# A decoder block: one weight's low half ordered behind the first pair's row maxima and the forget sums' copy, and 11 of 16 residual transfers issued by GpSimd

## The chip, the cores and the metric

The kernel runs on one core of a Trainium2 chip. Its time is the device time of one execution, in microseconds (us). A profiled execution is traced as well; its span is the time from the first to the last traced instruction.

The core's engines are named as in the profile: PE (TensorE, matrix products; PEld is its loading of the stationary operand), DVE (VectorE), ACT (ScalarE), POOL (GpSimd) and SP (SyncE, which here only issues DMAs). Each engine works through its own queue in order and waits for others by semaphores.

## The reference

One layer of a hybrid decoder block, in fp32, for one sequence of 256 tokens with 1024 channels:

```python
h = rms_norm(x, attn_norm_g)
proj = h @ w_in        # q, k, v of two branches (8 heads of 64 each), forget logits, gate logits
qa, ka = partial_rope(rms_norm(heads(qa))), partial_rope(rms_norm(heads(ka)))
o_a = moba_attention(qa, ka, va)                 # blocks of 256 keys
log_f = log_sigmoid(f_logit + b_forget); c = cumsum(log_f)
o_b = softmax(rms_norm(qb) @ rms_norm(kb).T / 8 + c[t] - c[s], causal) @ vb
gates = sigmoid(g_logit + b_gate)                # two branches of 1024
merged = gates[0] * (o_a @ w_branch_moba) + gates[1] * (o_b @ w_branch_fox)
x = x + merged @ w_out
h2 = rms_norm(x, ffn_norm_g)
u, g = split(h2 @ w_ffn_up)                      # 2 x 2816
x = x + (silu(causal_depthwise_conv3(g) + b) * u) @ w_ffn_down
```

With 256 tokens there is a single block of keys, so the MoBA branch is plain causal attention.

## The kernel before

**Weights in two halves.** Every product with a weight is made of two fp32r numbers for each fp32 number: a high half and a low half. A weight chunk is 1 MB. SP loads it in one DMA into a raw buffer (`raw`, three of them, L131). Each half of the chunk (1024 of its 2048 columns) is then split: ACT copies it to `whi` (L134), and DVE subtracts that from the raw chunk and writes `wlo` (L135). Three products (high·high, high·low, low·high) are summed in PSUM. The halves `whi` and `wlo` rotate through six buffers each.

**What sets the order.** PE works in the order in which the program is written. The orders of DVE, ACT, SP and POOL are made by the scheduler of the framework from the program's order, its dependences and its own estimates. `load(upto)` (L116) walks through a fixed list of chunks (the projections, then gate weights wg 0 to 7, then the branch, output and feed-forward weights) and emits loads and splits up to half number `upto`. `use(c, h)` (L143) is called by each product group for its weight; unless `state["hold"]` is set, it first calls `load` five halves (AHEAD) beyond its own. `state["behind"]` may name two instructions behind which the next splits' high and low half are ordered (`after`, L89): this adds an order on the queue, but no data.

**The stage around the first edit.** `project(n, ..)` (products L247) makes the n-th projection; its last argument picks quarters of it. In the old program `project(4, pk, 1)` is the second half of the second key projection. Behind it come `forget_c` (L359 to L370: four products with a constant matrix sum the log forget gates, DVE copies them out of their PSUM bank, L366, adds a constant, L367, and ACT's queue sends them out and back in by two DMAs, L369 and L370), and `scores(0, pair)`, three of the four pairs of heads of the first branch. A pair's scores are `first_half` (products L400) and `second_half` (L407; L413 for the forgetting branch), then `softmax` (L420 to L437): DVE takes the row maxima (L428), ACT the exponentials (L431), DVE the reciprocal (L433) and the scaling (L436). PSUM has eight banks, so products wait for whoever reads a bank out.

Behind that, `finish_qk` normalises the second queries and keys (reduction L262, small operations L200 to L205, final product L269), and `start_turn` (L288 to L299) turns them: DVE transposes 32 by 32 blocks (L293), and 16 DMAs of 32 KB, issued by POOL and SP in turn, move the blocks (L298). Then come `project(5)` (the second values), `gate(0)` (products into two banks, evacuated by DVE at L490), the turn of the first pairs' probabilities (`turn`, products L450, evacuations L440 and L452), and so on through the gates and the four pairs of the forgetting branch.

**The stage around the second edit.** Late in the kernel, `spread_x` (L729 to L732), called behind feed-forward tile 17, issues 16 DMAs that spread the turned residual `turned_x` into `x1`, 32 partitions at a time. `down` (L776 to L820) adds `x1` to the output products (L799 and L809) and stores. Behind these 16 on SP stand the last two loads of the down weights (`wd`, L131).

Of the kernel before, what the change touches and what calls it, by code (L numbers as in the profile page):

```python
# [30 lines left out]
RB, HB, AHEAD = 3, 6, 5  # L31
# [11 lines left out]
def decoder_block(ctx, tc, a, out):  # L43
    nc = tc.nc
# [6 lines left out]
    def T(shape, tag, bufs=1, dt=F32):  # L51
        return sb.tile(shape, dt, tag=tag, bufs=bufs, name=tag)
# [32 lines left out]
    pos = {c: i for i, c in enumerate(chunks)}  # L85
    split = {}
    state = {"next": 0, "raw": None, "ahead": AHEAD, "hold": False, "behind": None}

    def after(i, j):  # L89
        tc.add_manual_dep(i.ins, j.ins.name, mybir.DependencyInfo(mybir.DependencyClass.NoSync, mybir.DependencyReason.DATA), reason="order")  # L90

    def lead(p):

        for k in (2 * p, 2 * p + 1):
            nc.sync.dma_start(lt[:, k], a["lead"][k])
        hi = T([P, 1024], "whi", HB, F32R)
        lo = T([P, 1024], "wlo", HB, F32R)
        for j in range(2):
            w = lt[:, 2 * p + j, S:]
            s = slice(j * W4, (j + 1) * W4)  # L100
            low = split_x(2 * p + j)
            whi = nc.scalar.activation(hi[:, s], w, AF.Copy)  # L102
            after(nc.vector.tensor_tensor(lo[:, s], w, hi[:, s].bitcast(F32), op=ALU.subtract), low)  # L103
        split[("qkv", 0, p // 2), p % 2] = (hi, lo, whi)

    def home(n):

        slot = (n - state["base"] - AHEAD - 1) % (HB + 3) if AHEAD < state["ahead"] else 3
        if slot > 2:
            return T([P, 1024], "whi", HB, F32R), T([P, 1024], "wlo", HB, F32R)  # L110
        if slot == 2:
            return [T([P, 1024], "qn", 3, F32R) for _ in range(2)]
        both = T([P, 2, 1024], ("V", "bias")[slot], 1, F32R)
        return both[:, 0], both[:, 1]

    def load(upto):  # L116
        while state["next"] <= min(upto, 2 * len(chunks) - 1):
            i, h = divmod(state["next"], 2)
            state["next"] += 1
            if i < 2:  # L120
                lead(2 * i + h)
                continue
            c = chunks[i]
            if h == 0:
                w = 1024 if i == 2 else 2048
                src = a[c[0]]
                for j in (c[1] - (c[0] == "qkv"), *c[2:]):
                    src = src[j]
                raw = state["raw"] = T([P, 2048], "raw", RB)
                for j in range(2048 // w):  # L130
                    nc.sync.dma_start(raw[:, j * w:(j + 1) * w], src[:, j * w:(j + 1) * w])  # L131
            raw = state["raw"][:, h * 1024:(h + 1) * 1024]
            hi, lo = home(2 * i + h)
            whi = nc.scalar.activation(hi, raw, AF.Copy)  # L134
            wlo = nc.vector.tensor_tensor(lo, raw, hi.bitcast(F32), op=ALU.subtract)  # L135
            if state["behind"]:
                for i, j in zip((whi, wlo), state["behind"]):
                    if j:
                        after(i, j)
            split[c, h] = (hi, lo, whi)  # L140
            state["whi"] = whi

    def use(c, h):  # L143
        if not state["hold"]:
            load(2 * pos[c] + h + state["ahead"])
        return split.pop((c, h))[:2]
# [60 lines left out]
    def pairs(ap):  # L207
        return ap.rearrange("p (a t) -> p t a", a=2)
# [29 lines left out]
    def project(m, pt, h, quarters=(0, 1)):  # L238
        for hh in quarters:
            wh, wl = use(("qkv", m, h) if isinstance(m, int) else m, hh)  # L240
            for k2 in range(2):
                k = 4 * h + 2 * hh + k2
                rh, rl = (pairs(w[:, k2 * 512:(k2 + 1) * 512]) for w in (wh, wl))
                parts = ((xh, rh), (xl, rh), (xh, rl)) if m == 0 else ((xh, rh), (xh, rl), (xl, rh))
                for i, (lhs, rhs) in enumerate(parts):
                    for t in range(NT):
                        nc.tensor.matmul(pt[t], lhs[:, k, t * P:(t + 1) * P], rhs, start=(k == 0 and i == 0), stop=(k == KT - 1 and i == 2))  # L247
# [53 lines left out]
    def end_turn(raw, br, isk, behind=None):  # L301
        dst = T([P, 4, S], f"{'qk'[isk]}T{br}")
        gain = col(C_QG + 2 * br + isk)
        i = nc.scalar.activation(dst.rearrange("p d (c i) -> p d c i", i=32), raw, AF.Copy, scale=gain)
        if behind:
            after(i, behind)
        turned[br, isk] = dst
# [51 lines left out]
    def forget_c():  # L359
        lf = fg["lf"]  # L360
        cp = bank()
        c0, c1 = (cp[:NH, t * P:(t + 1) * P] for t in range(NT))
        for t, c in enumerate((c0, c1)):
            nc.tensor.matmul(c, lf[:, t], tri, start=True, stop=True)
        cT = T([P, 2, 384], "pT", 4)[:NH, 0, 0:S]
        nc.vector.tensor_copy(cT, cp[:NH, 0:S])  # L366
        nc.vector.tensor_scalar_add(cT[:, P:S], cT[:, P:S], cT[:, P - 1:P])  # L367
        cd = dr.tile([NH, S], F32, name="cd")
        nc.scalar.dma_start(cd, cT)  # L369
        nc.scalar.dma_start(bias[:, :, P:P + S], bass.AP(tensor=cd.tensor, offset=cd.offset, ap=[[0, P], [S, NH], [1, S]]))  # L370
# [12 lines left out]
    last_max = []  # L383
# [12 lines left out]
    def first_half(br, pair, sps=None):  # L396
        sps = sps or banks()
        for j in range(2):
            rows = parts[j][0]
            nc.tensor.matmul(sps[j][:, 0:P], turned[br, 0][rows, pair, 0:P], turned[br, 1][rows, pair, 0:P], start=True, stop=True)  # L400
        return sps

    def second_half(br, pair, sps):
        if br not in halved:
            for j in range(2):
                rows = parts[j][0]
                nc.tensor.matmul(sps[j][:, P:3 * P], turned[br, 0][rows, pair, P:S], turned[br, 1][rows, pair], start=True, stop=True)  # L407
            return
        qs, ks = halved[br]
        for i, (q, k) in enumerate(((0, 0), (0, 1), (1, 0))):  # L410
            for j in range(2):
                rows = parts[j][0]
                nc.tensor.matmul(sps[j][:, P:3 * P], qs[q][rows, pair], ks[k][rows, pair], start=(i == 0), stop=(i == 2))  # L413

    def scores(br, pair):
        sps = first_half(br, pair)
        second_half(br, pair, sps)
        softmax(br, pair, sps)

    def softmax(br, pair, sps):  # L420
        s = T([P, 2, 384], "s", 4)
        nm = T([P, 2, 2], "nm", 4)
        l = T([P, 2, 2], "l", 4)
        for j in range(2):
            h = 2 * pair + j
            sp = sps[j]
            for i, c in enumerate((slice(0, 128), slice(128, 384))):
                last_max[:] = [nc.vector.tensor_tensor_reduce(s[:, j, c], sp[:, c], mask3[:, c] if br == 0 else bias[:, h, c],  # L428
                                               scale=1.0, scalar=3e38, op0=ALU.add, op1=ALU.min, accum_out=nm[:, j, i:i + 1])]
            for i, c in enumerate((slice(0, 128), slice(128, 384))):  # L430
                last_exp[:] = [nc.scalar.activation(s[:, j, c], s[:, j, c], AF.Exp, scale=-1.0, bias=nm[:, j, i:i + 1], accum_out=l[:, j, i:i + 1])]  # L431
        r = T([P, 2, 2], "r", 4)
        nc.vector.reciprocal(r, l)  # L433
        for j in range(2):
            for i, c in enumerate((slice(0, 128), slice(128, 384))):
                last_norm[:] = [nc.vector.tensor_scalar_mul(s[:, j, c], s[:, j, c], r[:, j, i:i + 1])]  # L436
        probs[br, pair] = s  # L437
# [60 lines left out]
    def banks():  # L498
        return [bank() for _ in range(NT)]

    forget_a()
    pq, pk, pv = banks(), banks(), banks()
# [17 lines left out]
    pk = banks()  # L520
# [1 line left out]
    gate_bias()  # L522
    end_turn(q0, 0, 0)
    end_turn(k0, 0, 1)
    project(4, pk, 1)
    forget_c()
    for pair in range(3):
        scores(0, pair)
    q1 = start_turn(q1, 0, last_norm[0])
    k1 = start_turn(finish_qk(pk, 1, 1, last_max[0]), 1)  # L530
# [192 lines left out]
    x1 = lt[:, :, S:2 * S]  # L723
    turned_x = lt[:, :, 2 * S:3 * S]
# [4 lines left out]
    def spread_x():  # L729
        for r in range(4):  # L730
            for b in range(4):
                nc.sync.dma_start(x1[32 * b:32 * (b + 1), r::4], turned_x[32 * r:32 * (r + 1), b::4])  # L732


    acts = {}
# [175 lines left out]
```

## Time and profile before

| | us |
|---|---|
| the three runs | 349.32, 349.60, 349.99 |
| their median | 349.60 |
| the profiled execution | 350.03 |
| its span | 348.3 |

The profiled execution's own time is 1.7 us more than its span. In the profile's rows a line stands for one group of instructions on one engine: its start in us from the span's start, its length, engine and line of the kernel, operation, what it writes and reads (with partitions x elements), and how many there were. A bracket at the end says how long the engine stood idle before the group, and what it waited for. In the chain of waits each row is a start, a length and what ran; the chain is followed back from the last instruction to whatever released it. In the windows each engine has its busy time in a stretch and in brackets its number of instructions; PEclk is the clock that PE was granted, as a share of full speed. A DMA issue's row is the time that the issuing engine's queue spends on it, and the rows of DMA issues give the median from issue to landing.

The engines' shares, the stretch around the edit and the end of the kernel are shown in the prediction, where they are used.

### The profile page before, as it was taken

How to read it: one execution, taken by the hardware profiler on the slowest of the kernel's cores; microseconds unless marked ns; L12 is line 12 of the kernel's file. 1: busy time of each engine (PE TensorE's matmuls, PEld its weight loads, DVE VectorE, ACT ScalarE, POOL GpSimd, SP SyncE). 2: the span in 40 equal slices, each digit the busy share in tenths (PEclk: the TensorE clock that was granted, in tenths of full speed). 3: DMA queues.
4: the chain of work that ended last, by engine and by line, in shares of the span. 5: the costliest groups of instructions: out<-in, count | busy, mean ns of one | idle time of the engine just before them, and what ended most of it. 6: DMA issues, size and time to landing. Idle time of an engine off the chain costs nothing.

```text
span 348.3 us, 5440 instructions
## 1 busy us (share of the span) xinstructions
PE 342.0 (98%) x1983; PEld 299.8 (86%) x1983; DVE 297.1 (85%) x562; ACT 222.3 (64%) x384; POOL 18.3 (5%) x40
## 2 busy tenths in 40 slices
PE   8999999899999999999999999999999999999995
PEld 4878888788888888889999999989898999989884
DVE  4899998999979678998999999897978988797833
ACT  4967656877589575746767877574765674566320
POOL 0000161044000000000000000000000000000000
PEclk9999999999999999999999999999999999999999
DMA  7987859757940927575626656566465755545003
GB/s 263 413 344 255 296 157 312 280 157 210 350 170 6 340 60 250 194 275 207 243 74 289 208 170 243 226 243 218 147 239 166 241 199 196 191 102 237 2 0 121
DMA packets 17994, 72.19 MB, mean 207 GB/s; under 512 B 2856, under 2 KB 8112, under 8 KB 10544
## 3 DMA queue, kind: packets, MB, share of 16 engines
q1 hardware_dynamic: 15744, 69.74, 56.5%
q0 software_dynamic: 1024, 1.05, 1.3%
q10 hardware_dynamic: 1200, 1.06, 0.9%
q8 instruction: 15, 0.25, 0.3%
q14 instruction: 11, 0.09, 0.1%
HBM read 67.64 MB, written 1.06 MB: 197 GB/s over the span
## 4 chain that ended last, share of the span: by engine, by line
PE 81%; DMA 9%; DVE 4%; ACT 2%; SPq 2%; issue 1%; ACTq 0%
PE bank L647 26%; PE bank L786 16%; PE bank L247 15%; PE bank L648 13%; PE bank L598 6%; DMA raw<-in_qkv 6%; DVE wlo L135 2%; SPq L298 2%; PE bank L464 2%; DMA lead<-in_lead 1%; DMA raw<-in_wg 1%; ACT whi L134 1%; PE bank L450 1%; ACT qn L180 1%; PE bank L413 0%
## 5 line engine op out<-in xcount | busy, mean ns | idle before, releaser
L135 DVE TENSOR_TENSOR wlo<-raw,whi 128x1024 fp32r<-128x1024 f32 x94 | 113.9, 1220 | 9.6 <-ACT whi L134 9.1
L134 ACT ACTIVATE whi<-raw 128x1024 fp32r<-128x1024 f32 x94 | 97.9, 1053 | 25.9 <-PE bank L647 6.8
L247 PE MATMUL bank<-whi,x 128*128 128x512 f32 x320 | 84.1, 382 | 0.6 <-ACT whi L102 0.5
L647 PE MATMUL bank<-pp,whi 128*128 128x512 f32 x232 | 76.6, 382 | 0.0
L247 PEld LDWEIGHTS bank<-whi,x 128*128 128x128 f32 x320 | 60.0, 189 | 11.1 <-ACT whi L102 1.2
L648 PE MATMUL bank<-pp,wlo 128*128 128x256 f32 x232 | 63.3, 273 | 0.0
L647 PEld LDWEIGHTS bank<-pp,whi 128*128 128x128 f32 x232 | 43.9, 189 | 6.1
L247 PE MATMUL bank<-wlo,x 128*128 128x512 f32 x160 | 47.9, 381 | 0.0
L648 PEld LDWEIGHTS bank<-pp,wlo 128*128 128x128 f32 x232 | 44.6, 192 | 0.2
L247 PEld LDWEIGHTS bank<-wlo,x 128*128 128x128 f32 x160 | 30.0, 189 | 4.8 <-DVE wlo L103 0.8
L786 PE MATMUL bank<-whi,qT 128*128 128x512 f32 (+1 forms) x92 | 27.8, 371 | 0.0
L755 DVE TENSOR_TENSOR sq<-bank,lows 128x256 f32<-128x256 f32 x44 | 18.1, 417 | 8.7 <-ACT lows L754 8.6
L760 ACT ACTIVATE s<-sq,sm 128x256 f32<-128x256 f32 x22 | 13.1, 597 | 12.1 <-DVE sq L756 11.9
L754 ACT ACTIVATE lows<-bank 128x256 f32<-128x256 f32 x44 | 16.0, 369 | 7.2 <-PE bank L648 7.2
L298 POOL DMA_DIRECT2D pp<-pp x32 | 17.0, 540 | 47.4 <-DVE qf L268 22.9
L786 PEld LDWEIGHTS bank<-whi,qT 128*128 128x128 f32 x92 | 17.3, 190 | 2.3
L763 ACT ACTIVATE s<-s 128x256 f32<-128x256 f32 x22 | 9.1, 413 | 15.6 <-DVE s L762 15.5
L647 PE MATMUL bank<-pp,bias 128*128 128x512 f32 x56 | 18.7, 382 | 0.0
L786 PE MATMUL bank<-wlo,qT 128*128 128x512 f32 (+1 forms) x46 | 17.0, 370 | 0.0
L598 PE MATMUL bank<-whi,pp 128*128 128x512 f32 x64 | 17.0, 383 | 0.0
L756 DVE TENSOR_TENSOR sq<-sq,rsB 128x512 f32<-128x512 f32 x22 | 15.2, 691 | 0.5
L431 ACT ACTIVATE s<-s,nm 128x128 f32<-128x128 f32 (+1 forms) x32 | 14.2, 451 | 1.8 <-DVE nm L428 1.8
(180 smaller groups left out, 578.3 us busy)
## 6 DMA issues: line engine op xcount, KB each, us to landing
raw<-in_wu SPq DMA_DIRECT2D x22, 1024.0 KB, 4.8
raw<-in_wd SPq DMA_DIRECT2D x11, 1024.0 KB, 4.7
raw<-in_qkv SPq DMA_DIRECT2D x9, 1024.0 KB, 6.3
raw<-in_wg SPq DMA_DIRECT2D x8, 1024.0 KB, 5.4
raw<-in_wb SPq DMA_DIRECT2D x4, 1024.0 KB, 5.3
raw<-in_wo SPq DMA_DIRECT2D x4, 1024.0 KB, 4.8
lead<-in_lead SPq DMA_DIRECT2D x8, 384.0 KB, 6.5
raw<-in_qkv SPq DMA_DIRECT2D x2, 512.0 KB, 8.2
```

What stands on the lines that cost most here:

```text
L134: whi = nc.scalar.activation(hi, raw, AF.Copy)
L135: wlo = nc.vector.tensor_tensor(lo, raw, hi.bitcast(F32), op=ALU.subtract)
L247: nc.tensor.matmul(pt[t], lhs[:, k, t * P:(t + 1) * P], rhs, start=(k == 0 and i == 0), stop=(k == KT - 1 and i == 2))
L298: queues[r % len(queues)].dma_start(raw[32 * r:32 * (r + 1), :, b], y[32 * b:32 * (b + 1), r])
L431: last_exp[:] = [nc.scalar.activation(s[:, j, c], s[:, j, c], AF.Exp, scale=-1.0, bias=nm[:, j, i:i + 1], accum_out=l[:, j, i:i + 1])]
L598: nc.tensor.matmul(ps_[t], lhs[:, t * P:(t + 1) * P], rhs, start=(k == 0 and i == 0), stop=(k == 3 and i == 2))
L647: nc.tensor.matmul(two[i], wh[:, c], both, start=(k == 0), stop=False)
L648: nc.tensor.matmul(two[i][:, 0:S], wl[:, c], high, start=False, stop=(k == KT - 1))
L754: nc.scalar.activation(lows[:, i:i + 1].rearrange("p b (a t) -> p b a t", a=2), apart(two[i][:, S:2 * S], 1), AF.Copy)
L755: nc.vector.tensor_tensor(halves(ev[:, i:i + 1]), apart(two[i][:, 0:S], 1), halves(lows[:, i:i + 1]), op=ALU.add)
L756: nc.vector.tensor_tensor(ev, ev, rs2[:, None, :].to_broadcast([P, 2, S]), op=ALU.mult)
L786: nc.tensor.matmul(o, lhs, rhs, start=(first and i == 0), stop=(end and i == 2))
```

## The change

Two places are edited. In the first, the second half of `project(4, pk, 1)` is written in two quarters, and before the second the loading ahead is held. So the split that `use` would have emitted there (the first half of gate weight 0) is not emitted until `forget_c` and the first pair's scores are written. Then it is emitted by hand, with its low half ordered behind `last_max[0]`, the last of the first pair's row maxima. Nothing is computed that was not before. In the second, of the 16 DMAs of `spread_x` five stay with SP and 11 are issued by GpSimd.

```diff
     end_turn(k0, 0, 1)
-    project(4, pk, 1)
+    project(4, pk, 1, (0,))
+    state["hold"] = True
+    project(4, pk, 1, (1,))
     forget_c()
-    for pair in range(3):
+    scores(0, 0)
+    state["hold"], state["behind"] = False, (None, last_max[0])
+    load(2 * pos["qkv", 4, 1] + 1 + AHEAD)
+    state["behind"] = None
+    for pair in range(1, 3):
         scores(0, pair)
...
         for r in range(4):
             for b in range(4):
-                nc.sync.dma_start(x1[32 * b:32 * (b + 1), r::4], turned_x[32 * r:32 * (r + 1), b::4])
+                (nc.sync if b == 3 or r == b == 0 else nc.gpsimd).dma_start(x1[32 * b:32 * (b + 1), r::4], turned_x[32 * r:32 * (r + 1), b::4])
```

The scheduler makes DVE's new order from that. The first piece is DVE's queue ahead of the copy of the forget sums (L366; `pT` is the buffer it goes to). A row is a line, an operation, what it writes and reads, its tile, and the semaphores for which it waits:

```order
 L269 TENSOR_TENSOR qn<-bank,qf 128x512 [waits DVE_49] x2
 L135 TENSOR_TENSOR wlo<-raw,whi 128x1024 [waits Activation_49]
-L135 TENSOR_TENSOR wlo<-raw,whi 128x1024 [waits DMAHW1_49,Activation_49]
 L366 COPY pT<-bank 8x256 [waits PE_49]
 L367 TENSOR_SCALAR pT<-pT 8x128 [waits DVE_49]
```

One low half has left its place in front of the copy. The one that stays is that of the last projection weight.

It comes back behind the first pair's maxima, where the low half of the same chunk's second half stood, and that one moves on behind the reduction (L262) of the second keys' normalisation. The next piece is DVE's queue there; `l` and `r` are the softmax's sums and reciprocals, `ss` and `qfv` the normalisation's small tiles:

```order
 L428 ISA nm 128x1
 L262 TENSOR_REDUCE ss<-sq 128x8 x2
+L135 TENSOR_TENSOR wlo<-raw,whi 128x1024
+L433 RECIPROCAL r<-l 128x4 [waits Activation_49]
 L200 TENSOR_SCALAR qfv<-ss 128x16 [waits DVE_49]
-L433 RECIPROCAL r<-l 128x4 [waits Activation_49]
 L436 TENSOR_SCALAR s<-s,r 128x128 [waits DVE_49]
```

The second half's low half now stands behind the two reductions, and one softmax's reciprocal and the first small operation of the normalisation have changed places.

PE's order is the same before and after. The last piece is PE's queue at the first two score products of the forgetting branch behind `gate(0)` to `gate(3)`, with the numbers of the buffers, since a bank's number tells who must have left it:

```order
L450 MATMUL bank_1125<-cst_172,s_974 128x64
L400 MATMUL bank_1140<-kT1_1067,qT1_997 128x128 [waits DVE_49,Activation_49]
L400 MATMUL bank_1141<-kT1_1067,qT1_997 128x128 [waits DVE_49]
L400 MATMUL bank_1144<-kT1_1067,qT1_997 128x128 [waits DVE_49]
L400 MATMUL bank_1145<-kT1_1067,qT1_997 128x128 [waits Activation_49]
L413 MATMUL bank_1140<-qn_1070,qn_1069 128x256
```

Four products start the first and second pair, each in a bank of its own, and each waits for the engine that read that bank out last.

On the two queues of the second edit, the 16 issues on SP become five ahead of the two `wd` loads, and POOL, which had nothing behind its 32 transfers of the turns (L298), gets eleven.

## The prediction

> **What bounds the kernel now.** I read the page's busy times first, then the windows, then the chain of waits in order of time around the edit, and then each engine's timeline there.
>
> ```profile
> PE 342.0 (98%) x1983; PEld 299.8 (86%) x1983; DVE 297.1 (85%) x562; ACT 222.3 (64%) x384; POOL 18.3 (5%) x40
> ...
> core 0: us, PE busy (x) PEld busy (x) DVE busy (x) ACT busy (x) POOL busy (x), PEclk, DMA share, GB/s
> 62.42:95.45 33.03, 32.96 (x178) 28.05 (x178) 32.89 (x86) 23.59 (x53) 8.43 (x16) 1.00 0.75 241
> 95.45:123.60 28.15, 28.15 (x198) 24.09 (x196) 20.90 (x67) 20.95 (x52) 0.00 (x0) 1.00 0.46 170
> ```
>
> TensorE (PE) is busy for 342.0 of the 348.3 us, at full clock, so a gain must come out of the 6.3 us in which it is not, or out of products that start late. From 62.42 to 95.45 us VectorE (DVE) is just as full, 32.89 of 33.03 us. There two engines bound the stage at once. After 95.45 only PE does. The chain shows how that stage is entered:
>
> ```profile
> 59.55 1.07 ACT whi L134
> 60.64 1.23 DVE wlo L135
> 61.86 0.33 DVE pT L366
> 62.22 0.28 DVE pT L367
> ...
> 63.65 15.59 PE bank L247 x71
> ```
>
> These are start, length and what ran. A weight's high half (ACT, L134) is waited for by its low half (DVE, L135), which stands in front of the copy of the forget sums (L366) on DVE, and PE's product stream resumes only at 63.65. The timelines of PE and DVE say why:
>
> ```profile
> 58.98 0.60 PE L364 MATMUL bank<-cst,lf 128*8 128x128 f32 x4
> 59.84 0.60 PE L407 MATMUL bank<-kT,qT 64*128 64x256 f32 x4
> 60.92 0.38 PE L400 MATMUL bank<-kT,qT 64*128 64x128 f32 x2
> 62.24 0.37 PE L400 MATMUL bank<-kT,qT 64*128 64x128 f32 x1 [0.93 <-DVE pT L366]
> 79.98 0.44 PE L400 MATMUL bank<-kT,qT 64*128 64x128 f32 x4
> 80.79 0.70 PE L247 MATMUL bank<-whi,x 128*128 128x512 f32 x2
> ```
> ```profile
> 57.96 1.22 DVE L135 TENSOR_TENSOR wlo<-raw,whi 128x1024 fp32r<-128x1024 f32 x1
> 60.64 1.23 DVE L135 TENSOR_TENSOR wlo<-raw,whi 128x1024 fp32r<-128x1024 f32 x1 [1.46 <-ACT whi L134]
> 62.42 0.27 DVE L428 CUSTOM_DVE_ANT_0 s<-bank,cst 128x128 f32<-128x128 f32 x1
> 63.53 1.21 DVE L135 TENSOR_TENSOR wlo<-raw,whi 128x1024 fp32r<-128x1024 f32 x1
> 65.22 0.16 DVE L433 RECIPROCAL r<-l 128x4 f32<-128x4 f32 x1
> 67.87 1.26 DVE L262 TENSOR_REDUCE ss<-sq 128x8 f32<-128x512 f32 x2
> 69.16 0.17 DVE L200 TENSOR_SCALAR qfv<-ss 128x16 f32<-128x16 f32 x1
> ```
>
> The forget products end at 59.58, but DVE idles 1.46 us for a high half and then works on the low half. The copy therefore comes more than 2 us late, the third pair's second score product waits 0.93 us for the bank that it frees, and project(5)'s first two products wait for the first pair's row maxima (62.42 to 63.60).
>
> **The change, part by part.**
>
> **1. The low half moves behind (gain at the door).** Without it DVE is free at 57.96 + 1.22 = 59.18. The copy starts when the forget products end, 59.6, takes 0.4, the scalar add 0.2: 60.25. The first pair's scores end at 59.84 + 0.60 = 60.44, and its four maxima take 63.53 - 62.42 = 1.1: DVE lets project(5)'s second product go at about 61.65. PE, no longer held at the third pair, needs what the same eight products need later without a wait, 80.79 - 79.98 = 0.81: 60.92 + 0.81 = 61.73, and one product (15.59 / 72 = 0.22) later 61.95. Before, that product stood at 63.65. So PE runs 1.7 us earlier from here by PE's own rows, 2.0 by DVE's. Nothing is removed: the low half still costs its 1.2 us on DVE, and DVE is full up to 95.45. So the question is what DVE owes at the end of its full stretch.
>
> **2. What DVE owes.** The moved half (first half of gate weight 0) takes the place that the next one (its second half) had at 63.53, and that second half goes behind L262. From there on DVE has done the same work as before at each row. Its clock there depends on the waits in between. DVE reaches the first reciprocal (L433) early and waits for ScalarE's exponentials:
>
> ```profile
> 61.65 1.05 ACT L134 ACTIVATE whi<-raw 128x1024 fp32r<-128x1024 f32 x1
> 62.52 0.53 ACTq L369 DMA_DIRECT2D cd<-pT  x1
> 63.10 0.40 ACT L431 ACTIVATE s<-s,nm 128x128 f32<-128x128 f32 x1 [0.40 <-DVE nm L428]
> 64.78 0.18 ACT L431 ACTIVATION_READ_ACCUMULATOR s<-s,nm 128x1 f32 x1
> ```
>
> ACT cannot start them before its high half of 61.65 ends, 62.65. In the old kernel they waited until 63.10, behind the DMA issue of 62.52 to 63.05, which itself waited for the forget copy. Now that issue goes out while the high half runs. The four exponentials take 63.10 to 64.96, 1.86, so they end at 64.5 and the reciprocal runs then instead of at 65.22: 0.7 earlier. From there to L262 nothing changes (2.65 us). Behind it stands the extra low half, 1.2 us, less some 0.2 to 0.3, since the small waits between the reduction, L200 and L436 are now filled by it. DVE is then late by 1.2 - 0.7 - 0.3 = 0.2 us, and stays so, being full. Bounds: 0.1 (exponentials at once) and 0.5 (nothing filled). If the exponentials started no earlier than before, it would be 1.0.
>
> **3. Where DVE and PE meet again.**
>
> ```profile
> 94.31 1.22 DVE L135 TENSOR_TENSOR wlo<-raw,whi 128x1024 fp32r<-128x1024 f32 x1
> 96.42 0.75 DVE L490 SCALAR_TENSOR_TENSOR lead<-bank,rs,lows 128x512 f32<-128x512 f32 x1 [0.89 <-PE bank L247]
> ...
> 97.39 0.30 PEld L400 LDWEIGHTS bank<-kT,qT 64*128 64x128 f32 x3
> ...
> 124.27 0.87 ACT L440 ACTIVATE pT<-bank 128x384 f32<-128x384 f32 x2 [5.64 <-PE bank L450]
> ...
> 123.54 0.75 DVE L490 SCALAR_TENSOR_TENSOR lead<-bank,rs,lows 128x512 f32<-128x512 f32 x1 [3.65 <-PE bank L247]
> ```
>
> Before, DVE had 0.89 us to spare at 96.42: the gate evacuation (L490) waited for PE. PE's first scores of the second forgetting pair, the middle one of the three rows from 97.39, at 97.5, reuse the bank that L490's first instruction frees. With PE 1.7 to 2.0 early, DVE arrives last: 95.5 + 0.2 = 95.7, plus 0.75 is 96.4. PE's product moves from 97.5 to 96.4. **1.1 us is left**, 0.8 with DVE 0.5 late. At 123.5 and 124.3 both other engines wait for PE by 3.65 and 5.64 us, so what PE has gained by then shifts everything behind it.
>
> **4. The next raw load.** The second half frees its raw buffer, so gate weight 3's load, issued at 64.76, moves behind L262, to about 69.5.
>
> ```profile
> 64.76 0.33 SPq L131 DMA_DIRECT2D raw<-in_wg  x1
> ...
> 76.69 1.06 ACT L134 ACTIVATE whi<-raw 128x1024 fp32r<-128x1024 f32 x1 [0.60 <-PE bank L247]
> ...
> raw<-in_wg SPq DMA_DIRECT2D x8, 1024.0 KB, 5.4
> ```
>
> It lands at about 75, and its conversion, at 76.69 before, waited for PE and not for data. Nothing is queued behind it on ACT that PE needs before the turn at about 77.5. I take 0.
>
> **5. The residual transfers.**
>
> ```profile
> 301.05 10.94 SPq L732 DMA_DIRECT2D lead<-lead  x16
> 312.08 1.01 SPq L131 DMA_DIRECT2D raw<-in_wd  x2
> ...
> 79.69 4.21 POOL L298 DMA_DIRECT2D pp<-pp  x8 [2.09 <-issue]
> ...
> pp<-pp POOLq DMA_DIRECT2D x32, 32.0 KB, 3.7
> ...
> 329.09 0.68 DVE L799 TENSOR_TENSOR s<-bank,lead 128x512 f32<-128x512 f32 x1
> ...
> 333.00 0.42 DVE L755 TENSOR_TENSOR sq<-bank,lows 128x256 f32<-128x256 f32 x1 [2.89 <-ACT lows L754]
> ```
>
> SP is free after 5 x 0.68 = 3.4 us instead of 10.94, so the last two weight loads go out some 5 to 8 us earlier. PE has no wait in that stretch, so this earns 0. GpSimd (POOL) issues 11; the trace has no such transfer from it. Bounds: 4.21 / 8 = 0.53 us each as for its own (5.8 us), or SP's 0.68 (7.5 us). I take 0.53. With 3.7 to land they are in by 311, and L799 reads them first at 329.09. The cover is 18 us; cost 0.
>
> That row also speaks to a rule. POOL's 0.53 us were taken at 79.69 to 83.9, beside a VectorE that was busy without a break. The Trainium skill (SBUF — State Buffer, "SBUF: two separate sides") says that descriptors of a GpSimd DMA cannot be written while VectorE holds the port pair that the two share. The same page, under "A bandwidth-pool intuition that's wrong (but worth ruling out)", gives about 620 ns alone and about 3100 ns beside such an operation. By that, as an estimate from this page, the eleven would take 34 us and come after L799. The trace speaks against it for this kernel's VectorE work.
>
> **Sum.** 1.1 + 0 + 0: span 348.3 to 347.2, this execution 350.03 to 348.9. It was 0.4 above the median of 349.6, to which I apply the same 1.1: 348.5 us.
>
> **Rivals.**
>
> *The whole gain stays:* the bank of L490 is not what PE waits for, and 1.7 to 2.0 us survive: 347.6 to 347.9. For: only one row in the stretch ties PE to DVE. Against: the order of the program has that wait. 0.10.
>
> *DVE gives it all back:* the exponentials start no earlier, DVE is 1.0 or more late, and 0 to 0.6 is left: 349.0 to 349.6. For: DVE is full for 33 us, and a queue that full forgives nothing. Against: the 0.40 idle before 63.10. 0.20.
>
> *The change does not act:* PE's bank and maxima are held by something else and 63.65 stays: 349.6. Against: the 0.93 names L366. 0.05.
>
> *Slower: GpSimd starved beside VectorE.* In 300 to 330 VectorE runs 1.2 us low halves. If each issue waited for two of them, 0.53 + 2 x 1.22 = 3.0, the eleven end at 333 and land at 336.5; L799 sits at the head of VectorE's queue until then, 7.4 late, and the last activations behind it have 2.9 of slack (333.00): 4.5 lost, less 1.1: 353. It decides from (329.1 - 301.1 - 3.7) / 11 = 2.2 us per issue. Against: 0.53 in both stretches seen. 0.08.
>
> **How the numbers follow.** Forecast 0.57 (348.3 to 348.8), rivals 0.10, 0.20, 0.05, 0.08. This kernel's measurement can tell about 0.2%, 0.7 us, from no change. Forecast and whole gain are faster, the next two within it, the last slower: 0.67, 0.25, 0.08. The range 347.6 to 349.7 takes in everything from the whole gain to none and leaves out the starved case and a little noise, about 1 in 10.
>
> **What would show it.** Step 1: project(5) resumes at 61.7 to 61.95, and the 0.93 before L400 is gone. Step 2: the reciprocal at 64.5 with DVE idle before it, L293 and the first row-turn transfers within 0.5 us of where they were. Step 3: L490 at 95.7 with no idle before it, and a wait of PE on it near 96.4; if that wait is absent, the first rival holds. Step 5: eleven POOL issues in about 6 us, L799 without a wait. I am wrong if project(5) resumes after 63, if DVE is more than 1 us late at L293, or if L799 waits.

## The result and the profile after

| | before | after |
|---|---|---|
| median, us (12 runs each, side by side) | 349.65 | 347.86 |
| lowest and highest | 348.85, 352.38 | 347.28, 348.96 |
| profiled execution | 350.03 | 347.68 |
| its span | 348.3 | 345.9 |

The ratio is 0.9946, with a 95% interval of 0.9927 to 0.9964: the kernel is 1.3 to 2.6 us faster. The forecast was 348.5, and the time lies within the range of 347.6 to 349.7. Two executions, of 398.64 us (the kernel before, beside the second four experiments) and of 926.5 us (the transfers alone), are left out of all ratios. The two profiled executions differ by 2.4 us of span, more than the medians (1.79). Most of what follows is about why.

The busy times of the changed kernel and its windows (columns as before), moved to where the same products now stand:

```profile
PE 341.7 (99%) x1983; PEld 299.9 (87%) x1983; DVE 296.4 (86%) x562; ACT 220.5 (64%) x384; POOL 24.2 (7%) x51
```
```profile
61.73:94.79 33.06, 33.06 (x178) 28.33 (x176) 32.78 (x78) 23.14 (x53) 8.44 (x16) 1.00 0.72 240
94.79:121.88 27.09, 27.09 (x193) 23.40 (x192) 20.81 (x67) 20.96 (x52) 0.00 (x0) 1.00 0.48 176
```

PE works as long as before, at the same full clock, in a shorter span; only waiting has gone. VectorE (DVE) is still full in the first window, 32.78 of 33.06 us. The timelines of PE at the two places of the prediction, the door of project(5) and the first scores behind `gate(0)` to `gate(3)`:

```profile
59.03 0.60 PE L364 MATMUL bank<-cst,lf 128*8 128x128 f32 x4
...
61.20 0.60 PE L407 MATMUL bank<-kT,qT 64*128 64x256 f32 x4
61.73 0.70 PE L247 MATMUL bank<-whi,x 128*128 128x512 f32 x2
...
77.47 0.96 PE L450 MATMUL bank<-cst,s 64*128 64x64 f32 x24
...
95.61 0.73 PE L400 MATMUL bank<-kT,qT 64*128 64x128 f32 x7
```

No row here carries a bracket: the 0.93 us before L400 has gone, and so has the wait that stood in front of project(5). At 95.61 PE does not wait either, though the prediction had it wait for L490 until 96.4. VectorE's timeline has the other side:

```profile
59.67 0.41 DVE L366 COPY pT<-bank 8x256 f32<-8x256 f32 x1 [1.45 <-PE bank L364]
...
61.64 1.22 DVE L135 TENSOR_TENSOR wlo<-raw,whi 128x1024 fp32r<-128x1024 f32 x1
...
63.62 0.18 DVE L433 RECIPROCAL r<-l 128x4 f32<-128x4 f32 x1 [0.21 <-ACT s L431]
...
67.47 1.21 DVE L135 TENSOR_TENSOR wlo<-raw,whi 128x1024 fp32r<-128x1024 f32 x1
...
70.85 1.30 DVE L293 STREAM_TRANSPOSE pp<-qn 128x512 f32<-128x512 f32 x2
...
94.79 1.41 DVE L490 SCALAR_TENSOR_TENSOR lead<-bank,rs,lows 128x512 f32<-128x512 f32 x2
```

The copy (L366) now waits for the forget products alone, the moved low half follows the maxima at 61.64, and the next one the reduction at 67.47. That is the order that the change asked for. But the reciprocal is at 63.62, where 64.5 was predicted, and L490 at 94.79, where 95.7 was predicted: VectorE is 0.9 us earlier than I had worked out, and the two L490 have ended just in time for PE. The second surprise is the end of the kernel. From the start of the last addition (L819 before, L825 after) to the end of the span it took 348.3 - 344.34 = 3.96 us before and takes 345.9 - 342.62 = 3.28 now:

```profile
344.34 0.42 DVE L819 TENSOR_TENSOR s<-bank,s 128x256 f32<-128x256 f32 x1 [0.92 <-PE bank L786]
```
```profile
342.62 0.42 DVE L825 TENSOR_TENSOR s<-bank,s 128x256 f32<-128x256 f32 x1 [0.92 <-PE bank L792]
```

So the 2.4 us between the two spans are 1.72 in which PE is earlier all the way to that addition, and 0.68 behind it. The prediction had 1.1 and 0.

### The profile page after: what moved, and what is told of

The parts are those of the page before. It is cut to its first block, busy times and chain, and to the rows that moved or that the text cites. A ratio compares the mean times of both kernels' runs of the same rounds, so it can differ in the third digit from the quotient of the medians.

```text
span 345.9 us, 5459 instructions
## 1 busy us (share of the span) xinstructions
PE 341.7 (99%) x1983; PEld 299.9 (87%) x1983; DVE 296.4 (86%) x562; ACT 220.5 (64%) x384; POOL 24.2 (7%) x51
## 4 chain that ended last, share of the span: by engine, by line
PE 99%; DVE 0%; issue 0%
PE bank L247 30%; PE bank L653 26%; PE bank L792 17%; PE bank L654 13%; PE bank L604 6%; PE bank L464 2%; PE bank L171 1%; PE bank L450 1%; PE bank L400 1%; PE bank L407 1%; PE bank L413 0%; PE bank L618 0%; PE bank L326 0%; PE bank L364 0%; DVE s L825 0%; PE bank L719 0%
## 5 line engine op out<-in xcount | busy, mean ns | idle before, releaser
L738 POOL DMA_DIRECT2D lead<-lead x11 | 5.8, 536 | 219.4 <-DVE lead L733 219.3
L298 POOL DMA_DIRECT2D pp<-pp x32 | 17.1, 542 | 46.8 <-DVE qf L268 22.1
```

Of the source, the lines that this page charges most:

```text
L298: queues[r % len(queues)].dma_start(raw[32 * r:32 * (r + 1), :, b], y[32 * b:32 * (b + 1), r])
```

## The experiments

Each kernel was timed beside the kernel before, which had medians of 349.63 (first four experiments), 349.28 (next four), 349.60 (next three) and 349.22 us (the last one). The transfers alone, the three and eight moved transfers and the first of the late ScalarE start from the old kernel, the others from the changed one. In the expectations e1 is the low half alone, e2 the transfers alone, e4 the extra subtraction, e6 the eight moved transfers, e8 L490 put first without that subtraction, and e10 and e11 the late ScalarE in the changed kernel, without and with L490 first. A ratio is to the kernel before, with its 95% interval.

### The two edits apart

```diff
-                (nc.sync if b == 3 or r == b == 0 else nc.gpsimd).dma_start(x1[32 * b:32 * (b + 1), r::4], ...)
+                nc.sync.dma_start(x1[32 * b:32 * (b + 1), r::4], ...)
```

> The low half's new place alone; all 16 residual transfers stay on SP. Theory A (the gain comes from the entry of project(5) alone): PE's product stream stands 1.7 us earlier from project(5) to the end, as in the changed kernel, and the time is the changed kernel's, 347.9 us, 0.5% below before. Rival (the residual transfers carry part of it, since the last two weight loads go out earlier): less, 348.5 to 349.3.

And the other edit alone, in the old kernel:

```diff
-                nc.sync.dma_start(x1[32 * b:32 * (b + 1), r::4], ...)
+                (nc.sync if b == 3 or r == b == 0 else nc.gpsimd).dma_start(x1[32 * b:32 * (b + 1), r::4], ...)
```

> Only the 11 residual transfers on GpSimd; the low half stays in front of the forget sums' copy. Theory A: nothing, 349.65 us; 11 issues by GpSimd at 0.53 us each, no wait of the final adds. Rival: 0.4 to 1 us faster, 348.6 to 349.2. The trace also shows a second time what the old order costs at the entry of project(5): theory A says that the cost depends on when a raw load of the first 35 us lands; with that load on time (its high half at 31.5 instead of 33.4) the copy comes 0.85 us sooner and PE loses 0.9 instead of 1.7 us there.

Measured: the low half alone 348.31 us, ratio 0.9965 [0.9952, 0.9978]; the transfers alone 348.54, 0.9969 [0.9953, 0.9986]. **Both edits earn**, 1.32 and 1.09 us against 349.63. The second, which I had put at 0, is not free of effect. Together they would give 0.9934, which lies within the interval of the change itself.

The traces say where. With the low half alone PE stands as in the changed kernel up to the last addition (342.69), and the end takes 346.6 - 342.69 = 3.9 us, as before. With the transfers alone the end takes 346.8 - 343.37 = 3.4. But that kernel's first part was faster than the profiled execution of before as well, with the old order. Its rows on ACT, on VectorE and on PE:

```profile
31.49 1.06 ACT L134 ACTIVATE whi<-raw 128x1024 fp32r<-128x1024 f32 x1 [0.16 <-DMA raw<-in_qkv]
```
```profile
59.69 1.23 DVE L135 TENSOR_TENSOR wlo<-raw,whi 128x1024 fp32r<-128x1024 f32 x1 [1.68 <-ACT whi L134]
60.83 0.41 DVE L366 COPY pT<-bank 8x256 f32<-8x256 f32 x1
```
```profile
62.16 1.04 PE L247 MATMUL bank<-whi,x 128*128 128x512 f32 x2
```

The copy still stands behind the low half, but it starts at 60.83, and 61.78 in the profiled execution of before. The reason lies 30 us earlier. The same row of ACT in before and in the changed kernel:

```profile
33.36 2.01 ACT L134 ACTIVATE whi<-raw 128x1024 fp32r<-128x1024 f32 x2 [2.07 <-DMA raw<-in_qkv]
```
```profile
31.49 1.06 ACT L134 ACTIVATE whi<-raw 128x1024 fp32r<-128x1024 f32 x1 [0.27 <-DMA raw<-in_qkv]
```

In the profiled execution of before, one load of a projection weight came 1.9 us late, though it was issued at the same time (26.47 and 26.40 us). ACT waited for it, and the low half behind it came 0.84 us late on VectorE (34.45, and 33.61 in the changed kernel). VectorE was still 0.96 late at 57.96 (57.00). ACT had caught up by 39 us, but at the door it was late again, at 59.55 (58.68), for a gate weight's load that had been issued 0.94 us later (54.59, 53.65). Neither edit acts as early as 31 us. In the other thirteen traces, of either order, the same high half starts at 30.93 to 31.82 us. So the late load is that execution's own, and the prediction took its times for the kernel's.

This sizes the door. From the forget products (L364) to the turn (L450), PE's rows are 20.20 us apart with the old order and the late load, 19.14 with the old order and the load on time (the transfers alone), and 18.44 in the changed kernel. The turn of before, and of the transfers alone the forget products, the turn and the last addition:

```profile
79.18 0.97 PE L450 MATMUL bank<-cst,s 64*128 64x64 f32 x24
```
```profile
59.09 0.60 PE L364 MATMUL bank<-cst,lf 128*8 128x128 f32 x4
```
```profile
78.23 0.96 PE L450 MATMUL bank<-cst,s 64*128 64x64 f32 x24
```
```profile
343.37 0.42 DVE L819 TENSOR_TENSOR s<-bank,s 128x256 f32<-128x256 f32 x1 [0.92 <-PE bank L786]
```

The low half's old place costs 1.76 us in the first case and **0.70 in the second**, which is also what is left at the last addition (343.37 - 342.62 = 0.75). The two other traces of the old order with nothing added on ACT, those of three and of eight moved transfers below, give 0.59 and 0.89.

Behind the turn the transfers earn nothing: from L450 to the last addition it takes 265.14 to 265.16 us in before, in the changed kernel, and with 11, three or eight transfers moved in the old one.

### Is it the forget copy alone, or the maxima too?

The low half goes behind the addition (L367) that follows the copy, so ahead of the first pair's maxima.

```diff
-        nc.vector.tensor_scalar_add(cT[:, P:S], ...)
+        fg["added"] = nc.vector.tensor_scalar_add(cT[:, P:S], ...)
...
-    scores(0, 0)
-    state["hold"], state["behind"] = False, (None, last_max[0])
+    state["hold"], state["behind"] = False, (None, fg["added"])
     load(2 * pos["qkv", 4, 1] + 1 + AHEAD)
     state["behind"] = None
-    for pair in range(1, 3):
+    for pair in range(3):
```

> The low half is ordered behind the forget sums' copy and add only, so it stands in front of the first pair's row maxima. Theory A (project(5) also waits for those maxima): the maxima end at 61.6 + 1.1 = 62.7, and project(5)'s second product starts there instead of at 61.95, 0.75 later; PE then keeps 1.0 of its 1.7 us: 348.6 us. Rival (only the bank that the copy frees counts): as the changed kernel, 347.9 us, with project(5) at 61.7.

Measured: 348.44 us, 0.9965 [0.995, 0.998]. VectorE's and PE's timelines:

```profile
60.29 1.21 DVE L135 TENSOR_TENSOR wlo<-raw,whi 128x1024 fp32r<-128x1024 f32 x1
61.43 0.27 DVE L428 CUSTOM_DVE_ANT_0 s<-bank,cst 128x128 f32<-128x128 f32 x1
```
```profile
62.11 1.04 PE L247 MATMUL bank<-whi,x 128*128 128x512 f32 x2 [0.34 <-DVE nm L428]
```

The copy comes out at once, the third pair runs without a wait, and now the maxima hold project(5). PE reaches L450 at 78.18, 0.71 later than in the changed kernel. That is what the old order costs with the load on time. So freeing the copy alone earns nothing at the door; both halves of step 1 were needed.

### Is L490 what ties PE to VectorE?

One more subtraction of 1.2 us on VectorE, shortly ahead of L490 (it writes the same numbers again):

```diff
-        halved[br] = qs, ks
+        halved[br] = qs, ks; nc.vector.tensor_tensor(ks[1], k, ks[0].bitcast(F32), op=ALU.subtract)
```

> The changed kernel with one subtraction of the forgetting branch's split keys done twice on VectorE (1.2 us more, the same result), shortly ahead of the gate's evacuation. Theory A (PE's first scores of the second forgetting pair wait for the evacuation's first instruction, and the changed kernel has only 0.25 us to spare there): the evacuation starts at 96.0 instead of 94.8, its first instruction ends at 96.7, PE shows a wait of about 0.95 us there for it, and the time is 348.8 us. Rival (that row does not tie PE to VectorE): 347.9 us and no wait.

Measured: 348.73 us, 0.9979 [0.9963, 0.9995]. VectorE and PE:

```profile
95.99 1.40 DVE L490 SCALAR_TENSOR_TENSOR lead<-bank,rs,lows 128x512 f32<-128x512 f32 x2
```
```profile
96.79 0.49 PE L400 MATMUL bank<-kT,qT 64*128 64x128 f32 x4 [0.74 <-DVE lead L490]
```

L490 comes 1.20 later, PE waits for it by 0.74, and the last addition is 0.83 later (343.45). So the wait that step 3 spoke of exists: 1.2 us more on VectorE cost 0.8 us. The changed kernel had only about 0.4 us to spare there.

Then the same subtraction, with L490 put ahead of the low half that stands before it:

```diff
+        halved[br] = qs, ks; nc.vector.tensor_tensor(ks[1], k, ks[0].bitcast(F32), op=ALU.subtract)
...
-                nc.vector.scalar_tensor_tensor(gates[t][g], ...)
+                state["evac"] = nc.vector.scalar_tensor_tensor(gates[t][g], ...)
...
-    gate(3, True)
+    state["hold"] = True; gate(3, True); state["behind"] = None, state["evac"]; load(2 * pos["wg", 3] + AHEAD); state["behind"] = None
```

> As e4 (the doubled subtraction of 1.2 us), but the last low half before the gate's evacuation is ordered behind it. Theory A (what PE waits for is the evacuation's place in VectorE's queue): the evacuation stands at 94.8 again, PE's wait of 0.74 us is gone, and the time is the changed kernel's, 347.9 us. Rival (any more work on VectorE in that stretch costs PE the same, since the maxima behind it come later too): as e4, 348.7 us.

Measured: 347.96 us, 0.9959 [0.9941, 0.9976]. VectorE and PE:

```profile
94.37 1.40 DVE L490 SCALAR_TENSOR_TENSOR lead<-bank,rs,lows 128x512 f32<-128x512 f32 x2
```
```profile
95.26 0.74 PE L400 MATMUL bank<-kT,qT 64*128 64x128 f32 x7
```

The same work costs nothing once L490 does not queue behind the low half. That order without the extra subtraction:

> The changed kernel with the last low half before the gate's evacuation ordered behind it. Theory A: PE has no wait for the evacuation in the changed kernel's trace (0.25 us to spare), so no gain in an execution whose loads land on time, 347.9 us; only executions in which VectorE comes late gain, so the upper runs come down by some tenths. Rival (the low half that moves is missed later, or the maxima behind it): 348.2 to 348.6 us.

Measured: 347.71 us, 0.9941 [0.9918, 0.9965]; L490 at 94.54, with 0.80 us of idle before it. It is not told apart from the changed kernel (0.9946), which had no wait of PE there to lose.

### The end of the kernel: which transfers, or how many?

The last addition is followed by an output DMA, and then SP waits until all DMAs have signalled. The trace's semaphore events show how: SP's DMAs signal eight semaphores in turn, and at the end SP passes nine waits in a fixed order. In each line, "place" is the wait that the last output DMA's semaphore belongs to; the times are us from the span's start, and the last three columns are the parts of the time behind the last addition's start.

```
kernel           x1 DMAs on SP  place  landed  first drain   to landing  to drain  to the end
before                16          4    346.68    347.43         2.34       0.75       0.87
low half only         16          4    345.03    345.75         2.34       0.72       0.85
transfers only         5          9    345.75    345.85         2.38       0.10       0.95
changed                5          9    344.99    345.09         2.37       0.10       0.81
```

Where the last DMA signals the fourth, SP still has six waits to pass behind its landing; where it signals the ninth, the other eight are done while it is under way. The rows of SP's waits in the profile, of before in the stretches 345.0 to 346.65 and 346.65 to 347.42, and of the changed kernel in 344.95 to 345.08 (minimum, median and maximum of one in ns, first and last start):

```profile
L907 SPq EVENT_SEMAPHORE  x3: 28/28/28, 345.2 to 345.7; - x3
```
```profile
L907 SPq EVENT_SEMAPHORE  x6: 28/28/28, 346.7 to 347.4; - x6
```
```profile
L913 SPq EVENT_SEMAPHORE  x1: 28/28/28, 345.0 to 345.0; - x1
```

If it is the place, it follows from the number of SP's DMAs alone, modulo eight. Eleven fewer shift it by the same as three fewer, and eight fewer leave it alone. So I moved three, and then eight, of the transfers in the old kernel:

```diff
-                nc.sync.dma_start(x1[32 * b:32 * (b + 1), r::4], ...)
+                (nc.gpsimd if r == 0 and b < 3 else nc.sync).dma_start(x1[32 * b:32 * (b + 1), r::4], ...)
```

> The kernel before with 3 instead of 11 of the 16 residual transfers on GpSimd. Theory L (the traces of e1 and e2 suggest it): SP's hardware-queue transfers take eight completion semaphores in turn, and at the end SP waits for these in a fixed order. Before, the last output transfer has the fourth of that row and six more waits stand behind it, 0.65 us. With 11 transfers fewer, and likewise with 3 fewer, it has the last one, and those waits are over before it lands. So 3 give all of it: from the last landing to SP's drain 0.1 instead of 0.75 us, 0.65 us faster than before. Rival W (the two last weight loads that leave earlier bring it, or SP's freed time): 3 of 11 of it at most, 0.2 us.

```diff
-                nc.sync.dma_start(x1[32 * b:32 * (b + 1), r::4], ...)
+                (nc.gpsimd if b < 2 else nc.sync).dma_start(x1[32 * b:32 * (b + 1), r::4], ...)
```

> The kernel before with 8 of the 16 residual transfers on GpSimd: eight fewer leave the last output transfer on the semaphore that it had. Theory L: 0.75 us from the last landing to SP's drain as before, and no gain, 349.6 us. Rival W: 8 of 11 of the gain of e2, 0.5 to 0.8 us faster.

The rows of the waits behind the last landing, of three moved and of eight moved:

```profile
L907 SPq EVENT_SEMAPHORE  x1: 28/28/28, 346.0 to 346.0; - x1
```
```profile
L907 SPq EVENT_SEMAPHORE  x6: 28/28/28, 345.6 to 345.9; - x6
```

```
kernel           x1 DMAs on SP  place  landed  first drain   to landing  to drain  to the end
three moved           13          9    345.94    346.05         2.33       0.11       0.85
eight moved            8          4    345.55    345.98         2.34       0.43       1.12
```

In the trace the place decides as foretold: the end takes 346.9 - 343.61 = 3.3 us with three moved and 347.1 - 343.21 = 3.9 with eight. The six waits took only 0.43 us there and not 0.75, and what stands behind them 1.12; why is open. In time, three moved is 349.01 us, 0.9987 [0.9971, 1.0003], and eight moved 349.31, 0.9988 [0.9966, 1.0009]. The 0.3 between the medians has the right sign, but the ratios are the same, neither is told apart from no change, and the 0.65 foretold for three moved did not show. So **the trace shows the mechanism, and the timings alone don't**. What speaks for it in time is the whole second edit, at 0.9969, and its 1.09 us is more than the trace explains.

### A late ScalarE, made on purpose

Three kernels were to bring the late half of ACT back, by a second evacuation of the turned keys (L304), which writes the same numbers: in the old kernel, in the changed one, and in the one with L490 ahead.

```diff
-        if behind:
-            after(i, behind)
+        if behind: after(i, behind)
+        elif isk: nc.scalar.activation(dst.rearrange("p d (c i) -> p d c i", i=32), raw, AF.Copy, scale=gain)
```

> The kernel before with the turned keys' evacuation by ScalarE (1.15 us at about 57.5) done twice with the same result, so that its next high half comes about 0.85 us later: what a raw load that lands late did in the profiled execution of before. Theory A: in the old order the copy of the forget sums waits for that high half's low half, so it comes 0.85 us later than in e2 and e6 and PE loses 1.6 to 1.7 instead of 0.7 us at the entry of project(5): 0.9 us slower, 350.2 us. Rival (the old order's loss does not hang on that high half): as before, 349.3 to 349.6 us.

> The changed kernel with the same doubled evacuation. Theory A: the entry of project(5) is not touched, 61.7, but the first pair's exponentials start 0.85 us later (62.6 instead of 61.7), the first reciprocal stands at 64.5, the gate's evacuation at 95.6 instead of 94.8, and PE waits 0.5 us for it: the state that the prediction assumed, 348.4 us. Rival (VectorE makes up for it on the way): no wait, 347.9 us.

> e8 (evacuation ahead of the last low half) with the same doubled evacuation of the keys. Theory A: the evacuation no longer stands behind a late low half, so PE does not wait, and the lateness costs nothing: 347.8 us, 0.5 us below e10. Rival: the maxima behind the moved low half now make PE wait, 348.2 us or more.

Measured: 349.75 us, 0.9998 [0.998, 1.0016]; 347.93, 0.9953 [0.9937, 0.997]; 348.15, 0.996 [0.9945, 0.9975]. As timings they settle nothing. ACT's timeline of the second and PE's of the third:

```profile
56.62 1.15 ACT L304 ACTIVATE kT<-pp,sm 128x1024 f32<-128x1024 f32 x1 [1.55 <-DMA pp<-pp]
...
61.89 0.40 ACT L431 ACTIVATE s<-s,nm 128x128 f32<-128x128 f32 x1
```
```profile
60.54 0.49 PE L400 MATMUL bank<-kT,qT 64*128 64x128 f32 x4 [0.86 <-ACT kT L306]
```

In the second the turned blocks had landed 0.6 us earlier than in the changed kernel's trace (57.24), so the exponentials came at 61.89, hardly late (61.73). In the third PE itself waited for the doubled evacuation, a wait that the case doesn't have. In the old kernel project(5) came 0.87 us later than with the transfers alone (63.03, 62.16), but PE had started the forget products 0.33 later there (59.42, 59.09). In its trace the door costs 79.11 - 59.42 - 18.44 = 1.25 us, 0.55 more than with the load on time. The 0.9 us expected in time did not come: the time can't be told from that of before, and its interval ends at 0.56 us slower.

The dose was then given apart from the keys: five small copies on ACT into a buffer that nobody reads.

```diff
+        elif isk: spare = T([P, 192], "spare"); [nc.scalar.activation(spare, dst.rearrange("p d s -> p (d s)")[:, 0:192], AF.Copy) for _ in range(5)]
```

> The changed kernel with five small copies (128x192, into a tile of their own that nobody reads) on ScalarE between the turned keys' evacuation and the first pair's exponentials, four of them ahead of the high half there; unlike in e10 and e11, PE waits for none of them. They cost about 0.4 us each, so the exponentials start 1.2 to 1.9 us later than 61.7. Theory A (the lateness of the exponentials is carried by a VectorE without idle time to the gate's evacuation, and from 0.25 us on PE pays for it): the evacuation comes later than 94.8 by as much, PE shows a wait for it of 0.25 us less, 1.0 to 1.6 us, and the time is 348.9 to 349.5 us. Rival (VectorE makes it up in between): the evacuation at 95.1 or earlier, no wait, 347.9 us.

Measured: 348.03 us, 0.9967 [0.9955, 0.9979]. ACT, VectorE and PE:

```profile
62.56 0.38 ACT L431 ACTIVATE s<-s,nm 128x128 f32<-128x128 f32 x1
```
```profile
64.44 0.18 DVE L433 RECIPROCAL r<-l 128x4 f32<-128x4 f32 x1 [1.02 <-ACT s L431]
```
```profile
95.60 1.41 DVE L490 SCALAR_TENSOR_TENSOR lead<-bank,rs,lows 128x512 f32<-128x512 f32 x2
```
```profile
96.41 0.49 PE L400 MATMUL bank<-kT,qT 64*128 64x128 f32 x4 [0.35 <-DVE lead L490]
```

The lateness was smaller than expected (0.83 us, not 1.2 to 1.9), and so were PE's wait and the time. These are the rows of the prediction: the reciprocal at 64.5, L490 at 95.7, PE at 96.4 with a wait on it. With ACT's exponentials 0.83 us late, as the late load left them, the chain of steps 2 and 3 holds link by link to 0.1 us. PE ends 0.44 later than in the changed kernel (last addition at 343.06).

## Why the prediction was right, and where not

**Step 1 had the right mechanism, and its size only for the profiled pair.** project(5) was to start at 61.73 by PE's rows and starts at 61.73; the wait before L400 is gone. That both the copy and the maxima hold it was right too, as the run with the low half behind the copy alone shows. But the 1.7 us hold against the profiled execution of before alone, whose load was late.

**Steps 2 and 3 had the right mechanism and the wrong size.** "The four exponentials take 63.10 to 64.96, 1.86, so they end at 64.5" and "95.5 + 0.2 = 95.7" were worked out from ACT's times in the one profiled execution, and these were 0.9 us late from a load at 31 us. With the load on time the reciprocal is at 63.62 and L490 at 94.79, early enough that PE keeps all that it gains at the door. What VectorE owes was right: beside the old order with the load on time (the transfers alone) it is 0.28 late at L293 (70.85, 70.57) and 0.20 at L490, which there could have started at 95.47 - 0.88 = 94.59:

```profile
95.47 1.41 DVE L490 SCALAR_TENSOR_TENSOR lead<-bank,rs,lows 128x512 f32<-128x512 f32 x2 [0.88 <-PE bank L247]
```

So the 0.2 stands, and the 95.5 to which it was added is what was 0.9 too late. The term of the sum that was mis-sized is the 1.1 of step 3. In the profiled pair PE keeps 1.72. But about 1.0 of that is the late load, which only the execution of before had: with the load on time on both sides the door is worth 0.59 to 0.89, 0.70 with the transfers alone. The load is late in one of fourteen traces. How often it is in executions without a trace isn't known, so the door's share in the medians stays open between these, with the lower the likelier. The forecast also took 1.1 us from the median, as if every execution of before had the late load.

**Step 4 was right.** The load of gate weight 3 was issued at 68.75 (69.5 predicted), and its conversion at 74.98 waits 0.59 us for PE, not for data. It cost nothing.

**Step 5 was wrong.** "PE has no wait in that stretch, so this earns 0": true of that stretch, and of the weight loads that go out earlier. The eleven issues run as foretold, in the changed kernel's page, SP's timeline and VectorE's:

```profile
L738 POOL DMA_DIRECT2D lead<-lead x11 | 5.8, 536 | 219.4 <-DVE lead L733 219.3
```
```profile
302.01 3.29 SPq L738 DMA_DIRECT2D lead<-lead  x5
305.40 5.66 SPq L131 DMA_DIRECT2D raw<-in_wd  x2
```
```profile
329.83 0.69 DVE L805 TENSOR_TENSOR s<-bank,lead 128x512 f32<-128x512 f32 x1
```

What step 5 left out is that eleven DMAs fewer on SP change which semaphore the last output signals. That took 0.65 us off the end in the traces.

**Rivals.** "The whole gain stays" came true in its size (347.6 to 347.9, at 0.10), but not by its condition: L490's bank is what PE waits for, as the extra subtraction showed. PE had nothing to wait for only because VectorE was early. "DVE gives it all back" did not come: the exponentials went out as soon as the high half was done. GpSimd starved did not come either: 0.536 us per issue, where 2.2 were needed, with L805 not waiting. (The sum of that rival had a slip: 301.1 + 11 x 3.0 is 334, not 333, which makes 354 of its 353.) VectorE was busy for only 3.08 of the 6.10 us around these issues, though; the rule that was weighed there, of the Trainium skill (SBUF — State Buffer, "SBUF: two separate sides"), speaks of a VectorE operation that holds the port, and the row that answers it remains the one from the turns, 0.53 us per issue beside a full VectorE.

**So the forecast was near for a sum of two errors.** It had 1.1 + 0; the measured 1.79 lies between 0.70 + 0.65 = 1.35 (load on time) and 1.76 + 0.65 = 2.4 (load late in the kernel before alone). The lower one is what the traces with the load on time give, and the interval, 1.3 to 2.6, just takes it in; the 0.4 us between it and the medians stay unexplained. If the load is late in both, it would be about 344.34 - 343.06 = 1.28, and 0.65, so 1.9; that is argued from the run with the late ACT, and no trace of the changed kernel shows it. That the time came so near the forecast is luck in part: the late load made the door too dear, and the end was not in the sum.

## What to carry to other kernels

Before the times of one profiled execution are made terms of a sum, look for a wait on a DMA upstream that is longer than its neighbours' and ask whether the next execution will have it: here one such load made an order look worth 1.76 us instead of 0.70. Other traces of the same stretch answer it. When two engines are both nearly full, find the one instruction that ties them, and work out how early the waiting one must be there; here some 0.4 us to spare decided whether PE kept all that it had gained. And count what an edit does to the number of DMAs on a queue, since the closing waits are passed in a fixed order.

## What was not expected of the hardware

- One and the same load, issued at 26.47 and 26.40 us in two executions, was ready for ACT 1.9 us later in the one than in the other; it was late in one of fourteen traces.
- The closing waits of SP cost 0.10 to 0.11 us behind the last landing if the last output's semaphore is waited for last, and 0.43 to 0.75 us if five waits stand behind its own, though each of the instructions is 28 ns long and, in the profiled execution of before, the DMAs of the other seven semaphores had landed 0.9 us or more before the last.
